# Fifty short idle matmuls in the opening, and one load moved in front of the first stores, in an RMSNorm and matmul kernel

## The chip, the cores and the metric

The kernel runs on one core of a Trainium2 chip. The metric is the device time of one execution, in microseconds (us), as the median of several runs. A profile of one execution comes with it; its span, from the first to the last instruction, is a little shorter than the device time. The core has five engines: TensorE (PE in the profile, with PEld for its weight loads), VectorE (DVE), ScalarE (ACT), GpSimd (POOL) and SyncE (SP), which here only issues transfers. Sixteen DMA engines move the data.

## The reference

```python
x = randn(16, 1024, 512)          # float32, 16,384 rows of 512
gamma = ones(512)
weight = randn(512, 768) * 0.1
eps = 1e-5

rms = sqrt(mean(x ** 2, axis=-1, keepdims=True) + eps)
x_norm = x / rms * gamma
return matmul(x_norm, weight)      # float32, 16,384 rows of 768
```

The rows are read once (33.6 MB), the result is written once (50.3 MB), and the weights are 1.6 MB.

## The kernel before

The 16,384 rows are 128 tiles of 128 rows; two tiles are a pair (the loop's j). Gamma is folded into the weights once, and the division by rms is done after the matmul, as a scaling of each output row, so that the matmul needs only x in bf16, transposed. For each pair GpSimd casts x to bf16, TensorE transposes it two columns at a time as 32-bit words, VectorE copies the transposed words out of PSUM, and TensorE multiplies. ScalarE takes the sums of squares of x and scales the even tiles; VectorE scales the odd ones. The last four tiles of each group of 16, from tile 28 on, go another way: GpSimd casts all four at once and VectorE transposes them in blocks of 32 by 32, so TensorE has no transposes for them.

x lies in SBUF in two buffers of 16 tiles, the outputs in three buffers of 8 tiles. Each load or store covers a stretch of tiles:

```python
XG, OG = 16, 8
AHEAD = 20
x_first, x_size = stretches(XG, {0: [2, 2, 4, 8], **{g: [8, 8] for g in (1, 4, 5, 6, 7)}})
o_first, o_size = stretches(OG, {0: [2, 2, 4], 1: [4, 4], last: [4, 4]})
...
xin = ctx.enter_context(tc.tile_pool(name="xin", bufs=2))
xbp = ctx.enter_context(tc.tile_pool(name="xb", bufs=4))
outp = ctx.enter_context(tc.tile_pool(name="out", bufs=3))
...
starts = [i for i in range(NT) if x_first[i] == i]

def load_until(i):
    while starts and starts[0] < i:
        load(starts.pop(0))          # nc.sync.dma_start
```

All loads of x, the weights and all stores are issued by SyncE, in program order, on one queue. The casts of a pair and of four tiles:

```python
def cast(i, engine, n=1):
    ...
    engine.tensor_copy(out=xb_tiles[i // 2][:, i % 2:i % 2 + n, :], in_=held(x_tiles, XG, i, n))

def cast_quad(q):
    quads[q] = quad_in.tile([P, 4, D], BF16, name="xq")
    nc.gpsimd.tensor_copy(out=quads[q], in_=held(x_tiles, XG, 4 * q, 4))
    ...
```

The opening issues the first loads, and keeps TensorE busy with matmuls on a tile of zeros, into a PSUM tile that nothing reads, while the data are on their way:

```python
load_until(2)
load_weights(0)
load_weights(1)
load_until(2 * XG - 8)               # tiles 2 to 23
...
def warm_up(n):
    for _ in range(n):
        nc.tensor.matmul(out=spare[:, :WIDE], lhsT=warm[:, :P], rhs=warm, start=True, stop=True)
...
warm_up(6)
gp = tpsum.tile([P, 2, 2], F32, name="tp")
for c in range(2):
    nc.tensor.transpose(out=gp[:, c, :], in_=g_row[:, :, c], identity=ident_f[:2, :2])
...
cast(0, nc.gpsimd)
cast(1, nc.gpsimd)
cast(2, nc.gpsimd, 2)
norms(0, 2)
warm_up(4)
transpose_tile(0)
transpose_tile(1)
warm_up(2)
weights(0, nc.vector, 0, WIDE)
...                                  # tiles 0 and 1
```

Then the loop over the pairs. The transposes of pair j + 2 are spread between the matmuls of pair j:

```python
for j in range(1, NP):
    if j >= 4:
        load_until((2 * j + AHEAD + XG - 1) // XG * XG)
    if j + 3 < NP and quad_of(j + 3) is None:
        cast(2 * j + 6, nc.gpsimd, 2)
    if (2 * j + 2) % XG == 0 and 2 * j + 2 < NT:
        cast_quad((2 * j + 2 + XG - 4) // 4)
    elif 2 * j >= XG:
        move_quad(3)
    ...                              # norms
    if j in marks:                   # j = 54: four loads of 2 to 4 KB on 12 to 15
        mark(marks[j])               # partitions, into a tile that nothing reads
    ...                              # the choice of feed
    for i, engine in ((2 * j, nc.scalar), (2 * j + 1, nc.vector)):
        a = accumulator()
        matmuls(i, a, range(K), feed)
        finish_tile(i, a, engine)    # scale, and the store where a stretch ends
```

At j = 4 the loop issues the load of tiles 24 to 31; tiles 0 to 7 are finished by then, so their three stores stand ahead of it. At j = 7 it issues tiles 32 to 47, and in the same turn, after the cast of tiles 20 and 21, GpSimd gets the cast of the four tiles 28 to 31.

Of the kernel before, what the change touches and what calls it, by code (L numbers as in the profile page):

```python
# [18 lines left out]
def kernel(  # L19
# [8 lines left out]
    nc = tc.nc  # L28
    P = 128

    x = x.flatten_outer_dims()
    out = out.flatten_outer_dims()
# [5 lines left out]
    XG, OG = 16, 8  # L38
    AHEAD = 20
    WIDE = 512  # L40
# [39 lines left out]
    def load(i):  # L80
        if i // XG not in x_tiles:
            x_tiles[i // XG] = xin.tile([P, XG, D], F32, name="xt")
        nc.sync.dma_start(out=held(x_tiles, XG, i, x_size[i]), in_=rows(x, i, x_size[i]))  # L83
# [3 lines left out]
    def load_until(i):  # L87
        while starts and starts[0] < i:
            load(starts.pop(0))

    def cast(i, engine, n=1):
        if i // 2 not in xb_tiles:
            xb_tiles[i // 2] = xbp.tile([P, 2, D], BF16, name="xb")
        engine.tensor_copy(out=xb_tiles[i // 2][:, i % 2:i % 2 + n, :], in_=held(x_tiles, XG, i, n))  # L94
# [13 lines left out]
    def norms(i, n):  # L108
        ssq = stats.tile([P, 4], F32, name="ssq")
        for t in range(n):  # L110
            square(i + t, ssq[:, t:t + 1])
        root(i, n, ssq)
# [30 lines left out]
    def transpose_tile(i):  # L143
        for h in range(2):
            transpose_word(i // 2, i % 2, h)
        evac(i // 2, i % 2, 1)
# [6 lines left out]
    def quad_of(j):  # L153
        return j // 2 if (2 * j) % XG >= XG - 4 and 2 * j >= XG else None
# [4 lines that stand above are left out]
        turned = quad_out.tile([P, 4, 2, P, 2], BF16, name="xTq")  # L159
        for n in range(2):  # L160
            xT_tiles[2 * q + n] = turned[:, 2 * n:2 * n + 2]
        words = quads.pop(q).rearrange("p t d -> p (t d)").bitcast(F32).rearrange("p (a w) -> p a w", w=P)
        out_words = turned.rearrange("p t h m c -> p (t h m c)").bitcast(F32).rearrange("p (a m) -> p a m", m=P)
        for tokens in range(0, P, B):
            for features in range(0, P, B):
                quad_moves.append((out_words[features:features + B, :, tokens:tokens + B],
                                   words[tokens:tokens + B, :, features:features + B]))

    def move_quad(n):
        for _ in range(min(n, len(quad_moves))):  # L170
            dst, src = quad_moves.pop(0)
            nc.vector.transpose(out=dst, in_=src)  # L172

    def scale(engine, dst, src, r):
        if engine is nc.scalar:
            nc.scalar.mul(out=dst, in_=src, mul=r)  # L176
        else:
            nc.vector.tensor_single_scalar(out=dst, in_=src, scalar=r, op=mybir.AluOpType.mult)  # L178

    def accumulator():  # L180
        return opsum.tile([P, 2, WIDE], F32, name="ops").rearrange("p a b -> p (a b)")
# [16 lines left out]
    def matmuls(i, acc, ks, feed=None):  # L198
        for k in ks:
            matmul(i, k, acc, 0, WIDE)  # L200
            if feed:
                feed()
            matmul(i, k, acc, WIDE, O)

    def finish_tile(i, acc, engine):
        scale(engine, out_tile(i), acc[:, :O], rstd_of[i])
        store(i)


    def feeder(pairs, gaps, alone=False):  # L210
        queue = [(j, t, h) for j in pairs for t in range(2) for h in range(2)]
        calls = iter(gaps)

        def feed():
            for _ in range(next(calls)):
                j, t, h = queue.pop(0)
                transpose_word(j, t, h)
                if alone and h == 1:
                    evac(j, t, 1)
                elif (t, h) == (1, 1):  # L220
                    evac(j)
        return feed

    with tc.manual_schedule():
        g_row = singles.tile([2, P, 2], F32)
        nc.scalar.dma_start(out=g_row, in_=gamma.rearrange("(h w c) -> h w c", w=P, c=2))
        nc.scalar.preload_act_table(AF.Sqrt)  # L227
        wv = weight.rearrange("(h w c) o -> w h (c o)", w=P, c=2)
        w_f32 = singles.tile([P, K, O], F32)

        def load_weights(h):
            nc.sync.dma_start(out=w_f32[:, 2 * h:2 * h + 2, :].rearrange("p c o -> p (c o)"), in_=wv[:, h, :])  # L232

        load_until(2)
        load_weights(0)
        load_weights(1)
        load_until(2 * XG - 8)

        for _ in range(20):
            nc.sync.drain()  # L240


        warm = singles.tile([P, WIDE], BF16)
        nc.vector.memset(warm, 0.0)
        eps_sb = singles.tile([P, 1], F32)
        nc.vector.memset(eps_sb, float(eps))  # L246
        ident_f = singles.tile([P, P], F32)
        make_identity(nc, ident_f)
        spare = accumulator()

        def warm_up(n):
            for _ in range(n):
                nc.tensor.matmul(out=spare[:, :WIDE], lhsT=warm[:, :P], rhs=warm, start=True, stop=True)  # L253

        w_bf = singles.tile([P, K, O], BF16)

        def weights(k, engine, lo=0, hi=O):
            scale(engine, w_bf[:, k, lo:hi], w_f32[:, k, lo:hi], g_sb[:, k % 2, k // 2:k // 2 + 1])


        probe = singles.tile([16, 16 * 64], F32)

        def mark(counts):
            for k in counts:
                nc.sync.dma_start(out=probe[:k, 64 * k:64 * k + 4 * k], in_=x[:k, :4 * k])

        warm_up(6)
        gp = tpsum.tile([P, 2, 2], F32, name="tp")
        for c in range(2):
            nc.tensor.transpose(out=gp[:, c, :], in_=g_row[:, :, c], identity=ident_f[:2, :2])  # L270
        g_sb = singles.tile([P, 2, 2], F32)
        nc.vector.tensor_copy(out=g_sb, in_=gp)  # L272
        cast(0, nc.gpsimd)
        cast(1, nc.gpsimd)
        cast(2, nc.gpsimd, 2)
        norms(0, 2)
        warm_up(4)
        transpose_tile(0)
        transpose_tile(1)
        warm_up(2)  # L280
        weights(0, nc.vector, 0, WIDE)
        weights(0, nc.vector, WIDE, O)
        weights(1, nc.scalar)
        acc = [accumulator() for _ in range(2)]
        for i in range(2):
            matmuls(i, acc[i], [0, 1])
        weights(2, nc.vector)
        weights(3, nc.scalar)
        norms(2, 2)
        cast(4, nc.gpsimd)  # L290
        cast(5, nc.gpsimd)
        matmuls(0, acc[0], [2, 3])
        finish_tile(0, acc[0], nc.scalar)
        matmuls(1, acc[1], [2, 3], feeder([1], [2, 2], alone=True))
        finish_tile(1, acc[1], nc.vector)
        cast(6, nc.gpsimd, 2)

        mid, one, two, both = ([0, 0, 1, 1, 0, 1, 1, 0], [1, 1, 0, 1, 1, 0, 0, 0], [1, 0, 1, 0, 1, 0, 1, 0],
                               [1, 1, 1, 1, 1, 1, 1, 1])
        marks = {NP - 10: (12, 13, 14, 15)}  # L300
        for j in range(1, NP):
            if j >= 4:
                load_until((2 * j + AHEAD + XG - 1) // XG * XG)
            if j + 3 < NP and quad_of(j + 3) is None:
                cast(2 * j + 6, nc.gpsimd, 2)
            if (2 * j + 2) % XG == 0 and 2 * j + 2 < NT:
# [3 lines that stand above are left out]
            if j < 4:  # L310
                norms(2 * j + 2, 2)
            if 3 <= j < NP - 2:
                norms_by_four(j + 2)
            if j in marks:
                mark(marks[j])
            if j < 3:
                feed = feeder([j + 1], mid if j == 1 else one, alone=j == 1)
            elif j == 3:
                feed = feeder([4, 5], both)
            elif j + 2 < NP and quad_of(j + 2) is None:  # L320
                feed = feeder([j + 2], two)
            else:
                feed = None
# [3 lines that stand above are left out]
                finish_tile(i, a, engine)  # L327
# [35 lines left out]
```

## Time and profile before

| | before |
|---|---|
| time, median of 3 | 213.65 us (213.57 to 215.07) |
| span of the profile | 211.9 us |
| TensorE busy | 195.5 us (92%), 1,214 matmuls recorded |
| VectorE, ScalarE, GpSimd busy | 151.1, 149.4, 64.7 us |
| moved by DMA | 85.69 MB, 404 GB/s over the span |
| instruction queues q8, q14 | 9 packets (0.15 MB), 8 packets (0.07 MB) |
| the twelve idle matmuls | 5.5 us, 612 ns each |
| granted TensorE clock, mean | 0.976 |

The page's first part gives each engine's busy time; the second cuts the span in 40 slices of 5.3 us, with the busy share of each engine in tenths, the clock that TensorE was granted, and what the DMA engines moved. The chain, part 4, is followed back from the last instruction to what released it, step by step. A timeline line has start and duration in us, the engine, the line of the program, the operation, output and input, how many instructions are merged in it, and in brackets how long the engine was idle before it and what ended that. The trace has further records: each packet of the DMA engines with its start, duration and size, and the time of each semaphore update.

### The profile page before, as it was taken

What the parts mean: (1) busy time and instruction counts of PE and PEld (TensorE: products, weight loads), DVE (VectorE), ACT (ScalarE), POOL (GpSimd) and SP (SyncE); (2) the same over time, 40 slices, a digit from 0 to 9 for tenths busy, and PEclk for the clock granted to TensorE, in tenths of its full rate; (3) what the DMA queues carried; (4) which work ended last, traced back from release to release, by engine and by line L of the source; (5) the groups of instructions that cost most, each with busy time, mean ns of one, the idle gap of its engine ahead of it and who ended that gap; (6) DMA issues with size and microseconds to landing.
All of it is one profiled execution on the core that took longest, in us unless ns stands there. A gap on an engine that the chain in (4) does not pass through costs nothing.

```text
span 211.9 us, 3454 instructions
## 1 busy us (share of the span) xinstructions
PE 195.5 (92%) x1214; PEld 130.7 (62%) x1238; DVE 151.1 (71%) x270; ACT 149.4 (71%) x358; POOL 64.7 (31%) x65
## 2 busy tenths in 40 slices
PE   7899999399999999999999999999999999999910
PEld 2467776266677756776677667766667666776600
DVE  0465663589669985899579984999579975999410
ACT  4798778067877787787877787778877788778300
POOL 2247500904630084116230552105720266000000
PEclk9999999979999999999999999999999999999985
DMA  6999999997999999999999999999999999997994
GB/s 243 427 447 343 397 434 411 458 402 303 445 351 405 382 413 436 421 432 442 430 419 430 439 427 422 424 427 432 442 436 404 441 425 432 427 423 316 391 429 169
DMA packets 5601, 85.69 MB, mean 404 GB/s; under 512 B 718, under 2 KB 720, under 8 KB 1488
## 3 DMA queue, kind: packets, MB, share of 16 engines
q1 hardware_dynamic: 5580, 85.47, 96.3%
q8 instruction: 9, 0.15, 0.3%
q14 instruction: 8, 0.07, 0.1%
q10 hardware_dynamic: 4, 0.00, 0.0%
HBM read 35.14 MB, written 50.33 MB: 403 GB/s over the span
## 4 chain that ended last, share of the span: by engine, by line
PE 82%; issue 8%; DMA 3%; POOL 2%; SPq 1%; DVE 0%; POOLq 0%
PE ops L194 72%; PE tp L133 10%; DMA xt<-in_x_dram 3%; POOL xb L94 2%; DVE ot L178 0%; SPq L232 0%; SPq L83 0%; POOL xq L158 0%; POOLq L94 0%
## 5 line engine op out<-in xcount | busy, mean ns | idle before, releaser
L194 PE MATMUL ops<-w_bf,xT 128*128 128x256 bf16 (+1 forms) x783 | 148.2, 327 | 1.1 <-DVE w_bf L178 0.3
L194 PEld LDWEIGHTS <-xT 128*128 128x128 bf16 x800 | 78.9, 99 | 47.0 <-issue 1.9
L176 ACT ACTIVATE ot<-ops,rstd 128x768 f32<-128x768 f32 x64 | 57.7, 901 | 46.5 <-PE ops L194 46.0
L94 POOL CAST xb<-xt 128x1024 bf16<-128x1024 f32 (+1 forms) x52 | 51.2, 1009 | 95.7 <-DMA xt<-in_x_dram 49.8
L98 ACT ACTIVATE jk<-xt 128x512 bf16<-128x512 f32 x128 | 78.8, 619 | 2.1 <-DMA xt<-in_x_dram 2.1
L178 DVE TENSOR_SCALAR ot<-ops,rstd 128x768 f32<-128x768 f32 x64 | 64.6, 1009 | 9.7 <-PE ops L194 9.2
L133 PE MATMUL tp<-ident_f,xb 128*128 128x128 f32 x200 | 54.6, 278 | 3.8 <-POOL xb L94 3.7
L172 DVE STREAM_TRANSPOSE xTq<-xq 32x256 f32<-32x256 f32 x112 | 48.8, 436 | 6.4 <-POOL xq L158 4.4
L140 DVE COPY xT<-tp 128x1024 bf16<-128x1024 bf16 (+1 forms) x53 | 34.8, 656 | 25.4 <-PE tp L133 24.8
L194 PE MATMUL ops<-w_bf,xTq 128*128 128x256 bf16 (+1 forms) x217 | 42.4, 324 | 0.4
L133 PEld LDWEIGHTS tp<-ident_f,xb 128*128 128x128 f32 x200 | 28.6, 143 | 7.7 <-POOL xb L94 4.9
L194 PEld LDWEIGHTS <-xTq 128*128 128x128 bf16 x224 | 21.9, 98 | 12.4
L98 ACT ACTIVATION_READ_ACCUMULATOR jk<-xt 128x1 f32 x128 | 24.4, 190 | 0.0
L158 POOL CAST xq<-xt 128x2048 bf16<-128x2048 f32 x7 | 13.3, 1895 | 19.2 <-DMA xt<-in_x_dram 19.2
L102 ACT ACTIVATE rms<-ssq,eps_sb 128x4 f32<-128x4 f32 (+1 forms) x35 | 10.4, 297 | 1.1
L104 DVE RECIPROCAL rstd<-rms 128x4 f32<-128x4 f32 (+1 forms) x35 | 6.1, 176 | 6.4 <-ACT rms L102 5.6
L253 PE MATMUL ops<-warm 128*128 128x512 bf16 x12 | 5.5, 612 | 1.2 <-DVE eps_sb L246 1.2
L253 PEld LDWEIGHTS <-warm 128*128 128x128 bf16 x12 | 1.5, 137 | 2.9 <-issue 1.7
L176 ACT ACTIVATE w_bf<-w_f,g_sb 128x768 bf16<-128x768 f32 x2 | 1.9, 935 | 1.2 <-DMA w_f<-in_weight_dram 0.9
L272 DVE COPY g_sb<-tp 128x4 f32<-128x4 f32 x1 | 0.2, 161 | 3.2 <-PE tp L270 3.2
L227 ACT ACT_TABLE_LOAD x1 | 1.3, 1283 | 1.3 <-PEq L344 1.3
L178 DVE TENSOR_SCALAR w_bf<-w_f,g_sb 128x512 bf16<-128x512 f32 (+2 forms) x3 | 1.4, 481 | 0.1
(10 smaller groups left out, 1.9 us busy)
## 6 DMA issues: line engine op xcount, KB each, us to landing
out_dram<-ot SPq DMA_DIRECT2D x13, 3072.0 KB, 16.2
xt<-in_x_dram SPq DMA_DIRECT2D x11, 2048.0 KB, 18.1
xt<-in_x_dram SPq DMA_DIRECT2D x2, 4096.0 KB
out_dram<-ot SPq DMA_DIRECT2D x5, 1536.0 KB, 8.9
w_f<-in_weight_dram SPq DMA_DIRECT2D x2, 768.0 KB, 5.0
out_dram<-ot SPq DMA_DIRECT2D x2, 768.0 KB, 12.0
xt<-in_x_dram SPq DMA_DIRECT2D x2, 512.0 KB, 3.6
xt<-in_x_dram SPq DMA_DIRECT2D x1, 1024.0 KB
```

Of the source, the lines that this page charges most:

```text
L94: engine.tensor_copy(out=xb_tiles[i // 2][:, i % 2:i % 2 + n, :], in_=held(x_tiles, XG, i, n))
L98: nc.scalar.activation(out=jk, in_=held(x_tiles, XG, i)[:, 0, :], func=AF.Square, accum_out=ssq)
L102: nc.scalar.activation(out=rms[:, :n], in_=ssq[:, :n], func=AF.Sqrt, scale=1.0 / D, bias=eps_sb)
L104: nc.vector.reciprocal(out=rstd[:, :n], in_=rms[:, :n])
L133: nc.tensor.transpose(out=tp_tiles[j][:, t, h, :], in_=words[:, lo:lo + P], identity=ident_f)
L140: nc.vector.tensor_copy(out=dst[:, t:t + n, :], in_=src[:, t:t + n, :])
L158: nc.gpsimd.tensor_copy(out=quads[q], in_=held(x_tiles, XG, 4 * q, 4))
L172: nc.vector.transpose(out=dst, in_=src)
L176: nc.scalar.mul(out=dst, in_=src, mul=r)
L178: nc.vector.tensor_single_scalar(out=dst, in_=src, scalar=r, op=mybir.AluOpType.mult)
L194: nc.tensor.matmul(out=acc[:, lo:hi], lhsT=xT_tiles[i // 2][:, i % 2, k // 2, :, k % 2], rhs=w_bf[:, k, lo:hi], start=(k == 0), stop=(k == ...
L253: nc.tensor.matmul(out=spare[:, :WIDE], lhsT=warm[:, :P], rhs=warm, start=True, stop=True)
```

## The change

It has two parts. First, the load of tiles 24 to 31 goes back to the opening: all loads of the first two groups are issued before anything is stored, where before the last of them stood behind the stores of tiles 0 to 7. Second, the twelve idle matmuls of 512 columns become fifty of 128: 26, 18 and 6 in place of 6, 4 and 2. They keep TensorE busy for about as many columns, but are more instructions. Each matmul brings a weight load, so every later instruction of TensorE stands 76 places further back in its program, and the fetches of its instructions, which are transfers among the others, come at other moments. The computation is the same.

```diff
--- before.py
+++ after.py
@@ -234,7 +234,7 @@
         load_until(2)
         load_weights(0)
         load_weights(1)
-        load_until(2 * XG - 8)
+        load_until(2 * XG)
 
         for _ in range(20):
             nc.sync.drain()
@@ -248,9 +248,9 @@
         make_identity(nc, ident_f)
         spare = accumulator()
 
-        def warm_up(n):
+        def warm_up(n, columns=P):
             for _ in range(n):
-                nc.tensor.matmul(out=spare[:, :WIDE], lhsT=warm[:, :P], rhs=warm, start=True, stop=True)
+                nc.tensor.matmul(out=spare[:, :columns], lhsT=warm[:, :P], rhs=warm[:, :columns], start=True, stop=True)
 
         w_bf = singles.tile([P, K, O], BF16)
 
@@ -264,7 +264,7 @@
             for k in counts:
                 nc.sync.dma_start(out=probe[:k, 64 * k:64 * k + 4 * k], in_=x[:k, :4 * k])
 
-        warm_up(6)
+        warm_up(26)
         gp = tpsum.tile([P, 2, 2], F32, name="tp")
         for c in range(2):
             nc.tensor.transpose(out=gp[:, c, :], in_=g_row[:, :, c], identity=ident_f[:2, :2])
@@ -274,10 +274,10 @@
         cast(1, nc.gpsimd)
         cast(2, nc.gpsimd, 2)
         norms(0, 2)
-        warm_up(4)
+        warm_up(18)
         transpose_tile(0)
         transpose_tile(1)
-        warm_up(2)
+        warm_up(6)
         weights(0, nc.vector, 0, WIDE)
         weights(0, nc.vector, WIDE, O)
         weights(1, nc.scalar)
@@ -299,8 +299,7 @@
                                [1, 1, 1, 1, 1, 1, 1, 1])
         marks = {NP - 10: (12, 13, 14, 15)}
         for j in range(1, NP):
-            if j >= 4:
-                load_until((2 * j + AHEAD + XG - 1) // XG * XG)
+            load_until((2 * j + AHEAD + XG - 1) // XG * XG)
             if j + 3 < NP and quad_of(j + 3) is None:
                 cast(2 * j + 6, nc.gpsimd, 2)
             if (2 * j + 2) % XG == 0 and 2 * j + 2 < NT:
```

## The prediction

> **What bounds the kernel now.** I read the page first: part 2 for where TensorE and the DMA engines are not full, part 4 for the chain, part 3 for the queues.
>
> ```profile
> PE   7899999399999999999999999999999999999910
> DMA  6999999997999999999999999999999999997994
> ...
> q1 hardware_dynamic: 5580, 85.47, 96.3%
> q8 instruction: 9, 0.15, 0.3%
> ...
> PE 82%; issue 8%; DMA 3%; POOL 2%; SPq 1%; DVE 0%; POOLq 0%
> ```
>
> The chain names PE for 82%, and PE has only one hole, slice 7 (37.1 to 42.4 us). But DMA is full almost everywhere: the data queue's packets fill 96.3% of all 16 engines' time. Both could be the bound, so the hole and the DMA queue must be read in time. The hole, in the timelines of POOL and PE:
>
> ```profile
> 37.35 1.89 POOL L158 CAST xq<-xt 128x2048 bf16<-128x2048 f32 x1 [11.31 <-DMA xt<-in_x_dram]
> 39.19 3.01 POOL L94 CAST xb<-xt 128x1024 bf16<-128x1024 f32 x3
> ...
> 40.28 0.33 PE L133 MATMUL tp<-ident_f,xb 128*128 128x128 f32 x1 [3.40 <-POOL xb L94]
> ```
>
> GpSimd meets the quad cast of tiles 28 to 31 at 26.05 us and waits 11.31 us for their load, issued at 23.48 behind the stores of tiles 0 to 7. The cast of tiles 22 and 23, loaded long ago, stands behind it in program order and starts only at 39.19; TensorE waits 3.40 us for it. The windows around it (busy us per engine, granted clock, DMA share, GB/s):
>
> ```profile
> 36.00:40.00 4.00, 0.89 (x6) 0.36 (x4) 0.71 (x2) 1.31 (x5) 2.65 (x2) 1.00 1.06 453
> 40.00:44.00 4.00, 3.66 (x15) 2.27 (x17) 3.58 (x8) 1.84 (x4) 2.20 (x3) 0.67 0.99 429
> 44.00:48.00 4.00, 4.00 (x26) 2.70 (x24) 3.55 (x7) 2.02 (x7) 0.00 (x0) 0.90 0.97 411
> 48.00:52.00 4.00, 3.95 (x27) 2.70 (x27) 3.86 (x7) 3.05 (x9) 1.30 (x2) 1.00 0.82 347
> 52.00:56.00 4.00, 4.00 (x26) 2.35 (x24) 3.26 (x7) 3.16 (x8) 4.00 (x4) 1.00 0.74 313
> ```
>
> The stall also costs clock: after it PE runs at half clock from 41.36 to 44.77 (the trace's clock record), 3.4 us that are worth 1.7. So PE loses 3.4 + 1.7 = about 5.1 us. During the stall DMA is not disturbed (453 GB/s). It is disturbed later, at 48 to 56: the store of tiles 16 to 23, late because PE was late, is issued only at 52.49, when the queue has run dry. These windows count a packet where it starts; following the packets of each DMA engine one after another, I find nearly every engine idle for about 2.0 us from 51.4. That is all of the stall that DMA sees.
>
> The tail, in the same columns:
>
> ```profile
> 188.00:191.00 3.00, 2.95 (x21) 2.10 (x20) 2.91 (x7) 2.08 (x6) 0.00 (x0) 1.00 1.01 434
> 191.00:193.00 2.00, 2.00 (x15) 1.23 (x13) 1.94 (x3) 1.60 (x7) 0.00 (x0) 1.00 0.43 184
> 193.00:195.00 2.00, 2.00 (x14) 1.23 (x13) 1.91 (x6) 2.00 (x5) 0.00 (x0) 1.00 0.75 319
> ...
> 206.00:209.00 3.00, 0.00 (x0) 0.00 (x0) 0.00 (x0) 0.00 (x0) 0.00 (x0) 0.50 0.91 385
> ```
>
> Here most engines are idle again, 0.5 to 3 us from 191, but not all. A transfer updates its semaphore once per engine, and the updates of the last four stores (first engine, last engine) are 191.35 and 196.00; 201.73 and 203.52; 205.42 and 207.16; 209.10 and 210.81. The last engine's steps are 7.5, 3.6 and 3.65 us, and a 3 MB store takes 8 packets of 912 ns = 7.3 us on an engine, a 1.5 MB store 3.65: that engine never rests. The straggler of the 16, not the last matmul, sets the end.
>
> Why it lags: at the load of tiles 16 to 23 all updates lie between 22.04 and 22.88. At 23.31 comes the first packet of the instruction queue q8 (16,384 B, 961 ns), and the next store lands on 15 engines by 24.61, on one at 26.29: a lag of 1.7 us from one fetch. Nine such fetches come, one per about 248 recorded PE instructions, and they hit different engines.
>
> **What the Trainium skill says.** "DMA: Bandwidth & Descriptors", section "Why a DMA increments its semaphore by 16 and not by 1": the increments come from engines that finish independently, and only the full count means that all has landed. The spread above agrees. "Runtime: NRT & Kernel Launch", section "Instruction fetch mechanics": instructions arrive in 16 KiB blocks of 256, which the sequencer fetches ahead through a DMA queue of its own. The nine packets agree in size and spacing. "TensorE: Matmul & The Clock Gate", section "Part 1: The HAM clock gate", puts the array at half rate after an idle window of about 3.4 us; the 3,413 ns at half clock after the stall agree. Section "Wait — 56ns, not 53.3ns?" of that page gives 107 ns between matmuls of 128 columns at half clock; the trace has only 512 columns there, one per 427 ns, which is 107 per 128.
>
> **The change part by part.** *The load moved.* The load of tiles 24 to 31 is issued at about 4.2 us, right behind that of 16 to 23, which landed at 22.88. It takes 8 packets of 611 ns = 4.9 us, so it lands near 28, not 37.30. POOL's quad cast then waits some 2 us, not 11.3, ends near 30, and the cast of tiles 22 and 23 near 31; PE wants those at 36.9. The 3.40 us and the 1.7 of half clock go. Bytes and order of the rest stay: the stores of tiles 0 to 7 begin 4.9 us later (last landing of the third near 36, not 31.73), but their buffers are wanted only at tile 24, near 42. The load of tiles 32 to 47 has the same bytes before it as before, so it still lands near 50 (50.55 now). PE, 5.1 us earlier, would want its first cast near 51.3, and one cast takes 1.04: perhaps 0.4 us lost there.
>
> *DMA.* The store of tiles 16 to 23 is issued near 52.49 - 4.7 = 47.8, before the queue is dry. The 2.0 us of idle at 51.4 go. Nothing else in the DMA's time gets shorter: 61.9 MB still follow at the same 431 GB/s. From there all landings are 2.0 us earlier.
>
> *The tail.* PE gains 4.7 but DMA only 2.0, so the slack of output buffers shrinks by 2.7. The tightest is tile 112, whose buffer waits for the store of tiles 88 to 95: landed 180.65, wanted near 182.2, slack 1.5. It becomes a stall of about 1.2 us, which leaves PE 3.5 earlier: the last store is issued near 203.12 - 3.5 = 199.6. Free of backlog it would land 6.0 later (209.10 - 203.12), at 205.6. The straggler comes to 210.81 - 2.0 = 208.8, so DMA still sets the end and 1.5 of PE's gain is lost.
>
> *The matmuls.* 12 x 512 = 6,144 columns become 50 x 128 = 6,400. At half clock 26 take 2.8 us (6 took 2.74), 18 take 1.9 (4 took 1.89), 6 take 0.6 (2 took 0.85). Nothing on the opening's path, if the weight loads (137 to 150 ns each in the trace, beside the matmuls) still overlap at 107 ns. If they do not, up to 26 x 0.1 = 2.6 us are added, but the loads' queue does not see it, and PE has slack later.
>
> *The fetches.* 38 more matmuls and 38 more weight loads move each PE fetch 76 instructions earlier in the program: by the trace's count from 23.3 to about 18.0, 44.2 to 33.4, 183.1 to 177 (in the old time). The spacing of 248 puts a tenth near 196.6, old time, where there was none: up to 1 us on one engine near the end. I take a quarter of that as expected loss, and the same as expected gain from fetches that meet another engine. Sum: 213.65 - 2.0 = 211.6, and a little less, as the 0.5 to 3 us of rest at 191 leave some engines room: 211.4.
>
> **The rivals.** (a) *PE is the bound, as the chain says*: all 5.1 us come through, 208.5. For it: no PE wait after 60 us, and the last store is issued 1.1 us after the last matmul. Against it: the straggler's unbroken steps. (b) *The DMA is the bound and the stall was free*: the engine behind at 54.27 lost no time at 51, so if it, not one of the rested engines, sets the new end, the gain is nil, 213.6. For it: at 62.14 the updates of all engines lie within 0.63 us, so that lagging engine is not far ahead of the rested ones. Against it: the lag that counts at the end grew after 62, with the fetch at 65.38 (72.85 for 15 engines, 74.78 for one), on an engine that had rested. (c) *The fetches land well or badly*: each is worth about 1.7 us of lag on its engine; two on one engine, or the tenth on the straggler, give 213 to 214.5, and a spread over engines with slack 209.5.
>
> **Range and chances.** The centre is 211.4. Towards (a) I go to 209.3, towards (b) and (c) to 213.7. Faster by over 2% means under 209.4 and needs nearly all of PE's gain: 0.13. Slower by over 2% needs over 217.9, which only a new PE stall with half clock and a dry queue could make: 0.02. Within 2%: 0.85.
>
> **What would show it.** Right: no wait of PE on POOL near 40; no half clock between 8 us and the end; the store of tiles 16 to 23 issued near 48; no idle of DMA near 51; a new wait of ACT or DVE for an out buffer near tile 96 or 112; the last store issued 3 to 4 us earlier, and landing about 9 after issue instead of 7.7. Ten packets on q8, the first near 18. Wrong: the last landing earlier by 4 us or more (PE was the bound), or not at all (the straggler carries no gain), or the quad cast still waiting 10 us.

## The result

The changed kernel takes 210.62 us (median of 6, 210.49 to 210.88); the kernel before 213.67 (median of 6, 213.57 to 215.07). The ratio is 0.985 with a 95% interval of 0.982 to 0.987: about 3 us less, where 2.2 had been predicted.

From the page of the changed kernel, the same parts as in the prediction:

```profile
PE   7899999998999999999999999999999999999800
...
PEclk9999999999999999999999999999999999999985
DMA  6999999999999999999999999999999999997992
...
q1 hardware_dynamic: 5580, 85.47, 96.8%
q8 instruction: 10, 0.16, 0.3%
...
PE 81%; DMA 10%; DVE 2%; issue 1%; POOL 1%; SPq 0%; POOLq 0%
```

The hole of TensorE in slice 7 is gone, and the DMA's 7 in slice 9 is a 9. The chain still gives PE four fifths, although, as the experiments show, PE does not set the end. (Slices are counted from 0.) GpSimd's timeline now:

```profile
29.85 1.89 POOL L158 CAST xq<-xt 128x2048 bf16<-128x2048 f32 x1 [3.83 <-DMA xt<-in_x_dram]
31.69 3.01 POOL L94 CAST xb<-xt 128x1024 bf16<-128x1024 f32 x3
50.59 3.01 POOL L94 CAST xb<-xt 128x1024 bf16<-128x1024 f32 x3 [15.89 <-DMA xt<-in_x_dram]
```

The load of tiles 24 to 31 is in by 29.80, and the cast of tiles 22 and 23 starts at 31.69 in place of 39.19, before TensorE asks for it. The third line is the cast of tiles 32 to 37, which now waits for the load of 32 to 47 (last landing 50.44). In the windows (busy us of PE, PEld, DVE, ACT, POOL, granted clock, DMA share, GB/s) the stall and the half clock are gone:

```profile
36.00:40.00 4.00, 4.00 (x28) 2.84 (x28) 3.82 (x9) 3.08 (x9) 0.00 (x0) 1.00 1.05 452
40.00:44.00 4.00, 3.95 (x27) 2.74 (x27) 3.91 (x7) 2.72 (x8) 0.00 (x0) 1.00 0.99 428
44.00:48.00 4.00, 4.00 (x26) 2.56 (x26) 3.83 (x8) 3.35 (x8) 0.00 (x0) 1.00 0.99 421
48.00:52.00 4.00, 3.41 (x22) 1.96 (x21) 3.11 (x6) 3.49 (x10) 1.41 (x2) 1.00 1.03 438
52.00:56.00 4.00, 4.00 (x29) 2.75 (x27) 1.79 (x3) 2.31 (x6) 4.00 (x4) 1.00 1.04 443
```

PE loses only some 0.5 us at 51, and the DMA does not dip at 48 to 56. SyncE issues the store of tiles 16 to 23, and then the load of tiles 48 to 63, 5.2 to 5.4 us earlier than before; its timeline, first in the kernel before, then in the changed one:

```profile
52.49 0.33 SPq L191 DMA_DIRECT2D out_dram<-ot  x1
54.61 0.34 SPq L83 DMA_DIRECT2D xt<-in_x_dram  x1
```

```profile
47.28 0.33 SPq L191 DMA_DIRECT2D out_dram<-ot  x1
49.25 0.34 SPq L83 DMA_DIRECT2D xt<-in_x_dram  x1
```

The tail, in the columns of the windows above:

```profile
186.00:188.00 2.00, 2.00 (x14) 1.31 (x13) 1.91 (x5) 1.97 (x6) 0.00 (x0) 1.00 0.89 381
188.00:190.00 2.00, 1.95 (x13) 1.17 (x12) 1.94 (x4) 1.63 (x5) 0.00 (x0) 1.00 0.58 246
190.00:192.00 2.00, 2.00 (x14) 1.18 (x13) 1.80 (x5) 1.71 (x4) 0.00 (x0) 1.00 0.95 389
...
205.00:208.00 3.00, 0.00 (x0) 0.00 (x0) 0.00 (x0) 0.00 (x0) 0.00 (x0) 0.50 0.13 53
```

Most engines are through with their share near 188 and rest until the next store; in the last window only a few still move data. The last four stores land (first engine, last engine) at 187.48 and 193.10; 197.36 and 200.54; 201.09 and 204.20; 204.77 and 207.84. The last landings again lie 7.44, 3.66 and 3.64 us apart, where the packets alone take 7.3, 3.65 and 3.65: the engine that is last never rests. The end moved from 210.81 to 207.84. The last store was issued at 198.58, 4.5 us earlier than before; of that, 1.6 was lost behind the straggler.

### The profile page after: what moved, and what is told of

It is laid out like the page before. It is cut to its first block, busy times and chain, and to the rows that moved or that the text cites. A ratio compares the mean times of both kernels' runs of the same rounds, so it can differ in the third digit from the quotient of the medians.

```text
span 208.9 us, 3530 instructions
## 1 busy us (share of the span) xinstructions
PE 193.9 (93%) x1252; PEld 133.2 (64%) x1276; DVE 151.0 (72%) x270; ACT 149.2 (71%) x358; POOL 64.4 (31%) x65
## 4 chain that ended last, share of the span: by engine, by line
PE 81%; DMA 10%; DVE 2%; issue 1%; POOL 1%; SPq 0%; POOLq 0%
PE ops L194 69%; DMA xt<-in_x_dram 10%; PE tp L133 9%; PE ops L253 2%; DVE ot L178 1%; POOL xb L94 1%; DVE w_bf L178 0%; DVE xT L140 0%; SPq L191 0%; PE tp L270 0%; DVE warm L244 0%; POOLq L94 0%; DVE eps_sb L246 0%; SPq L83 0%
## 5 line engine op out<-in xcount | busy, mean ns | idle before, releaser
L194 PE MATMUL ops<-w_bf,xT 128*128 128x512 bf16 (+1 forms) x782 | 146.6, 325 | 1.5 <-DVE w_bf L178 0.6
L194 PEld LDWEIGHTS <-xT 128*128 128x128 bf16 x800 | 78.1, 98 | 46.1 <-issue 0.9
L194 PE MATMUL ops<-w_bf,xTq 128*128 128x512 bf16 (+1 forms) x218 | 42.5, 324 | 0.3
L253 PE MATMUL ops<-warm 128*128 128x128 bf16 x50 | 5.6, 302 | 1.2 <-DVE eps_sb L246 1.2
L253 PEld LDWEIGHTS <-warm 128*128 128x128 bf16 x50 | 5.0, 143 | 1.3 <-DVE eps_sb L246 1.2
```

Of the source, the lines that this page charges most:

```text
L194: nc.tensor.matmul(out=acc[:, lo:hi], lhsT=xT_tiles[i // 2][:, i % 2, k // 2, :, k % 2], rhs=w_bf[:, k, lo:hi], start=(k == 0), stop=(k == ...
L253: nc.tensor.matmul(out=spare[:, :columns], lhsT=warm[:, :P], rhs=warm[:, :columns], start=True, stop=True)
```

## The experiments

The theory: the end is set by the last of 16 DMA engines, and the gain is DMA idle time, caused through a late store by the PE stall. The rivals: TensorE sets the end, and its 5 us are the gain; or the places of TensorE's instruction fetches make it. In the later measurements the kernel before scattered more than in its first six runs (212 to 215.7 us). Two of the experiments scatter like it, by some 2 us: the two in which the DMA engines still rest near 51. The others scatter by 0.1 to 0.8 us, and small differences are taken between those. The name in brackets after each heading is the run's.

**Each part alone.** The load moved, with the twelve matmuls of 512 kept (load_alone, against the kernel before):

```diff
-        load_until(2 * XG - 8)
+        load_until(2 * XG)
...
-            if j >= 4:
-                load_until((2 * j + AHEAD + XG - 1) // XG * XG)
+            load_until((2 * j + AHEAD + XG - 1) // XG * XG)
```

> Only the load of tiles 24 to 31 moves to the opening; the twelve idle matmuls of 512 columns stay. Theory (the late load costs a PE stall, which makes a store late and leaves DMA idle for 2 us; that idle time is the gain): nearly the whole gain, 210.3 to 211.2 us, nine packets on q8, no PE wait near 40. Rival (the gain comes from where TensorE's fetches fall): near the time before, 212.8 to 213.7 us.

Measured: 210.71 us (210.33 to 211.09), ratio 0.985 (0.979 to 0.990). That is the whole gain. Its page has nine fetches:

```profile
q8 instruction: 9, 0.15, 0.3%
```

The fetches come at 21.95, 39.18 and so on, not at 17.84 and 34.06, and there is no tenth; its last landing is 207.94 against 207.84. So the fetches' places are worth nothing here that can be seen.

The fifty short matmuls, with the load left behind the stores (warm_alone):

```diff
-        load_until(2 * XG)
+        load_until(2 * XG - 8)
...
-            load_until((2 * j + AHEAD + XG - 1) // XG * XG)
+            if j >= 4:
+                load_until((2 * j + AHEAD + XG - 1) // XG * XG)
```

(this diff and those that follow are against the changed kernel, unless they say otherwise)

> Only the fifty matmuls of 128 columns; the load of tiles 24 to 31 stays behind the stores. Theory: the PE stall near 37 to 40 and the DMA idle time near 51 stay, so 213.0 to 214.3 us. Rival (fetch places make the gain): 210.5 to 212 us with the stall still there.

Measured: 212.99 us (211.64 to 214.10, one slow run of 216.81 left out), ratio 0.997 (0.994 to 0.999), at the lower edge of what the theory expected. The stall stays, but a little shorter: PE waits 2.6 us, not 3.4 (and still falls to half clock, from 40.12 to 43.54), because the late load's last landing is 36.22, not 37.30. The store of tiles 16 to 23 is issued at 51.41 instead of 52.49, and most engines idle 0.4 to 1.2 us near 51, not 2.0. The first fetch, at 17.38 here, leaves no lag: the load of tiles 16 to 23 lands between 22.21 and 22.77 and the next store between 24.11 and 24.69, where before one engine was at 26.29. So the fetches' places may matter as long as a stall hangs on a landing, but for some 0.5 us (the interval goes from 0.1 to 1.2). This rests on one profile of each kernel and is not tested further. Why this fetch left no lag, I only suppose: all engines were slowed near 19 to 21 in this kernel, and the engine with the fetch may have lost nothing more by it.

**The stall taken away without touching the queue** (late_quad). Against the kernel before; the loads and the matmuls are its own:

```diff
-            if (2 * j + 2) % XG == 0 and 2 * j + 2 < NT:
+            if j == 9:
+                cast_quad(7)
+            elif (2 * j + 2) % XG == 0 and 2 * j + 2 < NT and j != 7:
                 cast_quad((2 * j + 2 + XG - 4) // 4)
             elif 2 * j >= XG:
-                move_quad(3)
+                move_quad(4 if j < 14 else 3)
```

> The kernel before, its loads and idle matmuls untouched; only GpSimd's order changes: the cast of tiles 28 to 31 comes two pairs later, behind the casts of tiles 22 to 25. Theory (it is the stall in the casts' order, not the place of the load in the queue, that costs): the PE wait of 3.4 us goes, the store of tiles 16 to 23 is issued near 48, the DMA idle time near 51 goes, 210.3 to 211.3 us with the load still behind the stores. Rival (the load must stand in front of the stores, because the queue runs dry near 21 us otherwise): 212.5 to 213.7 us.

Measured: 210.74 us (210.66 to 210.78), ratio 0.985 (0.979 to 0.991), the same gain, with the load still issued at 23.91 behind the stores. The store of tiles 16 to 23 is issued at 48.46, and the DMA engines do not rest near 51 (429 GB/s from 48 to 52, 449 from 52 to 56). GpSimd's timeline:

```profile
27.69 1.04 POOL L94 CAST xb<-xt 128x1024 bf16<-128x1024 f32 x1 [1.87 <-PE tp L133]
38.40 1.04 POOL L94 CAST xb<-xt 128x1024 bf16<-128x1024 f32 x1 [9.67 <-DMA xt<-in_x_dram]
39.39 1.90 POOL L158 CAST xq<-xt 128x2048 bf16<-128x2048 f32 x1
```

GpSimd waits 9.67 us for the same load, but with tiles 22 and 23 already cast at 27.69, and TensorE does not stall near 40 (its longest wait is 1.8 us, for a transposed word of the quad). So the load's place in the DMA queue did not have to change. What cost was that a cast which waits stood in front of a cast that did not have to.

**TensorE made later** (pe_later). Before the matmuls of pair 25:

```diff
+            if j == 25:
+                idle = accumulator()
+                for _ in range(10):
+                    nc.tensor.matmul(out=idle[:, :WIDE], lhsT=warm[:, :P], rhs=warm, start=True, stop=True)
```

> The changed kernel with ten more idle matmuls of 512 columns at pair 25, some 2.15 us of TensorE's time. Theory (the DMA engines set the end, TensorE has slack): under 0.6 us of the 2.15 come through, 210.5 to 211.2 us. Rival (TensorE sets the end, as the chain says): all of it, 212.5 to 212.9 us.

Measured: 210.85 us (210.67 to 211.00), 0.2 more. In SyncE's timeline the last three stores begin at:

```profile
190.84 10.30 SPq L191 DMA_DIRECT2D out_dram<-ot  x3
```

The last is issued at 200.81, 2.2 us later than in the changed kernel, and lands at 207.82, in place of 207.84. So TensorE does not set the end, whatever share the chain gives it: it has at least 2.2 us to spare here.

**One store less** (one_store_less). The rows of tiles 0 and 1 are left out of the output:

```diff
-        if i == first + n - 1:
+        if i == first + n - 1 and first != 0:
```

> The changed kernel without the store of tiles 0 and 1 (768 KB, their rows of the output are left out). Theory (DMA engines saturated from the opening to the end): an engine saves 8 packets of 234 ns, 1.9 us, and the end comes 1.3 to 2.0 us earlier, 208.7 to 209.4 us. Rival (TensorE or a latency at the end is the bound): under 0.5 us, 210.1 to 210.7 us.

Measured: 208.75 us (208.64 to 209.30): 1.87 less, where 8 packets of 234 ns on each engine are 1.87. That the two agree to the hundredth is luck, with runs that scatter by 0.7 us; the profiled execution, the slowest of the four, has its last landing at 206.52, 1.3 us earlier. A transfer of the opening, taken away, moves the end by about its full length 180 us later: from there to the end the engine that sets it has no rest.

**The store made late** (store_late, then store_held). The first try put the store of tiles 16 to 23 behind tile 27 in the program:

> The changed kernel, but the store of tiles 16 to 23 is issued only after tile 27, some 5.9 us later (near 53, as in the kernel before) while TensorE runs without a stall. Theory (the gain is DMA idle time that went away): the DMA engines run dry near 51 again and the whole gain is lost though PE is 5 us ahead, 212.6 to 214.0 us. Rival (PE's 5 us are what was gained, by whatever way): 210.5 to 211.3 us.

Measured: 210.57 us, and nothing tested: the store was issued at 46.97, since an issue waits only for its own data, and SyncE had nothing else to do. In the second try SyncE first issues a copy that reads tile 27:

```diff
+        if i == 27:
+            nc.sync.dma_start(out=probe[:1, 0:4], in_=out_tile(27)[:1, :4])
+            nc.sync.dma_start(out=rows(out, 16, 8), in_=held(o_tiles, OG, 16, 8))
-        if i == first + n - 1:
+        if i == first + n - 1 and first != 16:
```

> The changed kernel with the store of tiles 16 to 23 truly held until tile 27 is finished: SyncE first issues a 16-byte copy that reads tile 27, then the store (the edit of store_late left the issue at 46.97 us, since an issue waits only for its own data). It should be issued near 53, as before the change, while TensorE is not stalled. Theory (the gain is DMA idle time that went away): idle near 51 for 2 to 2.7 us, 212.5 to 213.8 us; if the slow packets near 60 and 70 of the kernel before belong to that idle time, they come back too, and it is 213.2 or more. Rival (PE's 5 us are what was gained): 210.4 to 211.2 us.

Measured: 214.22 us (213.65 to 215.54); the kernel before took 214.33 beside it, a ratio of 1.001 (0.998 to 1.004). The whole gain is gone. SyncE's timeline and PE's waits of this run:

```profile
51.96 0.74 SPq L191 DMA_DIRECT2D probe<-ot  x1
52.81 0.34 SPq L192 DMA_DIRECT2D out_dram<-ot  x1
53.26 2.36 SPq L83 DMA_DIRECT2D xt<-in_x_dram  x1
```

```profile
PE tp L133 <- POOL xb L94: 2.2, 3, 1.0
PE ops L197 <- ACT ot L176: 1.3, 2, 0.9
```

The store is issued at 52.81 (52.49 before the change), and the next load, which stands behind it in SyncE's program, at 53.26 (54.61). TensorE has no wait over 1.0 us in the whole run beyond the opening, and full clock until its work ends. Most engines idle 2.2 to 2.9 us near 51. So what costs is that transfers are issued late, with or without a stall of TensorE; the run does not tell the late store from the late load. And something else comes back. Packets spread over their own time (GB/s in stretches of 4 us, worked out from the trace's packet records):

| from us | 48 | 52 | 56 | 60 | 64 | 68 |
|---|---|---|---|---|---|---|
| before | 374 | 294 | 421 | 339 | 428 | 347 |
| changed | 429 | 431 | 428 | 430 | 433 | 429 |
| store held | 343 | 254 | 426 | 343 | 431 | 350 |

The dip at 48 to 56 is the idle time. The dips at 60 and 68 are not: the engines are busy, but with packets that take 0.4 to 0.9 us longer than others of their size, on all engines at once. Following the packets of each engine, I find between 55 and 73 us, as the median of the 16 engines, 1.9 us of such excess before the change, 0.0 in the changed kernel, 1.9 with the store held, and 1.8 in warm_alone. The rest itself, near 51, is 1.9, 0.0, 2.5 and 0.8 us. So each of the three kernels that rest there loses nearly 2 us more to slow packets, however long the rest.

A rest is not needed for them, though. In one_store_less the engines do not rest near 51, and still the rate falls to 329 GB/s from 64 to 68, and the excess from 55 to 73 is 1.4 us on the median engine; that is the execution that took 0.5 to 0.7 us more than the other three.

**Fetches earlier still** (w64). 100 idle matmuls of 64 columns (52, 36 and 12):

> The changed kernel with 100 idle matmuls of 64 columns in place of fifty of 128: every fetch of TensorE's instructions comes another 100 instructions, some 8 us, earlier, with the same load order. Theory (where the fetches fall is worth little, because each one costs some DMA engine about as much): 210.3 to 211.1 us. Rival (their place is worth a microsecond or more): outside 209.8 to 211.5 us.

Measured: 210.70 us (210.62 to 210.87). The first fetch is at 9.19 and leaves its mark at once: the load of tiles 4 to 7 has its last landing at 12.94, not 11.82, for a first landing of 11.07. By the end this is no longer seen (last landing 208.02).

**The four small loads left out** (no_marks), and then the idle matmuls as well:

```diff
-            if j in marks:
-                mark(marks[j])
```

> The changed kernel without the four small loads at pair 54 into a tile that nothing reads. Theory (the last DMA engine sets the end, and each of these loads holds its engines for about 0.2 us, as the landings at 185 show): 0.2 to 0.8 us less, 209.8 to 210.4 us. Rival (they are too small to matter): 210.5 to 210.7 us.

Measured: 210.22 us (210.13 to 210.38), 0.4 less than the changed kernel's 210.62; no run of one lies within those of the other, nor within those of w64, measured beside it (210.62 to 210.87). Last landing 207.56, not 207.84. It beats both kernels, by an amount that fits the queue time of the four loads.

> The moved load with the old twelve idle matmuls, without the four small loads: nine fetches in place of ten, and elsewhere. Theory (each part of the fetches' places is worth little): 210.0 to 210.5 us, as no_marks (210.22). Rival (the tenth fetch, near the end, costs its microsecond): 209.3 to 209.8 us.

(no_marks_load: the edit of load_alone to the kernel before, and the small loads left out) Measured: 210.38 us (210.11 to 210.95), with nine fetches in place of ten. The tenth costs nothing that can be seen.

> no_marks without any of the idle matmuls: TensorE begins cold. Theory (DMA sets the end; TensorE has some 3 us to spare and the DMA queue is full with loads until 27 us): 210.0 to 210.6 us though TensorE loses 2 to 3 us in the opening. Rival (the idle matmuls pay): 211.5 us or more.

(no_warm: all three `warm_up` lines left out of no_marks) Measured: 210.40 us (210.01 to 210.59). Full clock comes at 11.28 us instead of 5.62, and the end is the same within the scatter: the idle matmuls of the opening, short or long, now buy nothing.

## Why the prediction was right, and where it was not

*The stall.* As predicted: the load landed at 29.80 ("near 28"), the cast of tiles 22 and 23 began at 31.69 ("near 31"), no half clock between 7.2 and 201.7 us, the store of tiles 16 to 23 at 47.28 ("near 47.8"), 0.5 us of PE lost to the load of tiles 32 to 47 ("perhaps 0.4").

*The clock.* Right that the half clock would go, but one reading was off: the 3,413 ns at half clock are how long the clock took to come back, not the idle time that lowered it. That was 3.40 us in the kernel before, and in warm_alone a wait of 2.62 us brought half clock too, so here less than the 3.4 us that the prediction cites was enough.

*The bound.* Right, and shown from both sides: 2.2 us added to PE changed the last landing by 0.02 us, 1.87 us of packets taken from each DMA engine changed the time by about as much. Rival (a), PE, is out. Rival (b), no gain because the lagging engine had not rested, is out as well: the last landing of the store of tiles 16 to 23 moved from 62.14 to 61.40 only, but that of the next load from 74.78 to 71.56.

*The size.* The term that was too small is the DMA's: 2.0 us predicted, 2.97 measured at the last landing. The step that failed is "Nothing else in the DMA's time gets shorter". I had taken the slow packets near 60 and 70, which the packet records showed, for part of the transfers, and left them standing. In this change they went with the idle time: on the median engine 1.9 us of each, and the median of the 16 landings of the load of tiles 48 to 63 moved by 3.8 us, from 72.55 to 68.73. With the store held both came back. The second part of the same step, "all landings are 2.0 us earlier", failed too. The landings did not move together: that load's last landing came 3.2 us earlier, and at the end the first landing of the last store came 4.3 us earlier (209.10 to 204.77) and the last 3.0, as the spread between the engines grew from 1.7 to 3.1. So the two terms make nearly 4 us, of which the last engine kept 3. That the centre of the prediction was only 0.8 us off is in part luck: the slow packets and the wider spread, neither of them foreseen, work against each other.

*The tail.* The stall for an out buffer came at the tile where it was expected, and is longer than predicted, but harmless. ScalarE's timeline in the changed kernel:

```profile
178.36 0.90 ACT L176 ACTIVATE ot<-ops,rstd 128x768 f32<-128x768 f32 x1 [2.53 <-DMA out_dram<-ot]
```

ScalarE waits 2.53 us for the store of tiles 88 to 95 (landed 178.27; 1.2 predicted), but TensorE has three accumulators, and the view of its waits after 60 us is empty: the last store is issued 4.54 us earlier, not 3.5. This does not touch the time, as the straggler comes later anyway. The last landing is 9.3 us after the last issue, against "about 9".

*The matmuls and the fetches.* 26, 18 and 6 took 2.95, 2.10 and 0.53 us (2.8, 1.9, 0.6 predicted): 113 and 117 ns each for the first two lots, so the weight loads of 143 ns do overlap. First fetch at 17.84 (18.0), the tenth at 190.81. I gave the fetches nothing on balance, and load_alone, w64 and no_marks_load bear that out; rival (c), with a microsecond either way, does not appear in any of them. What the change is named for did not make its gain.

*What stays open.* Why packets slow down on all engines at once: near 60 and 70 after the idle time, and in the opening at the end of the last load before the stores (19 to 21 in the kernel before, 24 to 28 in the changed one, 305 GB/s there). At those places loads give way to stores or stores to loads, and most engines are in step: 14 of 16 land within 0.6 us, while later in the run all 16 spread over 2 to 5.6 us. But being in step is not enough: in late_quad 14 of 16 land the store of tiles 16 to 23 within 0.55 us, a load comes next, and the rate does not dip (432 GB/s from 56 to 60, 430 from 60 to 64). Nor is it needed: in one_store_less 14 of 16 spread over 1.6 us at the landing before the dip. Nor do I know which engine a fetch will hit.

## What to carry to other kernels

Before believing a chain that names an engine, ask whether the transfers ever rest: landings per DMA engine, first and last, show a straggler that never does, and leaving out one early store tests it in one run. A stall of the compute engine then costs only what it causes in the DMA later, so look for the store that becomes late, for the idle time, and for slow packets after it. And on an in-order engine, put work that waits for a late load behind work that does not: here a new order of the casts, in a few lines, did as much as moving the load.

## What was not expected of the hardware

Three microseconds lie between the first and the last of 16 DMA engines at the end (204.77 and 207.84), and whichever engine is last works without a rest: the last landing of a 3 MB store comes 7.24 us after that of the store before it in the middle of the run (78.85 to 86.09), and 7.44 near the end (193.10 to 200.54), when most others have rested. A load of 2 to 4 KB costs each engine that takes part some 0.2 us of queue time (last landings 185.64, 185.85, 186.05, 186.24 for four in a row), far more than its bytes. And after 0.8 to 2.5 us of rest the median engine lost another 1.8 to 1.9 us to slower packets, in all three kernels where the engines had rested near 51; in one execution without a rest it lost 1.4.
